# Two modulation chunks of the last channel group: summed on VectorE instead of TensorE

## The chip, the cores and the metric

The kernel runs on one core of a Trainium2 chip, in one launch. The metric is the device time of that launch in microseconds. TensorE (PE in the profile) multiplies matrices, VectorE (DVE), ScalarE (ACT) and GpSimd (POOL) work on tiles, and SyncE (SP) issues all transfers from the chip's memory, in one queue.

## The reference

Two layers of a diffusion backbone over 256 latent and 256 context tokens of width 2048, in float32. What matters here is the start of the first layer:

```python
silu_c, silu_cc = jax.nn.silu(c), jax.nn.silu(c_ctx)
ml = (silu_c @ w_mod[i] + b_mod[i]).reshape(B, 6, 1, D)      # latent
mc = (silu_cc @ w_mod[i] + b_mod[i]).reshape(6, 1, 1, D)     # context
a_lat = modulate(rms_norm(h, norm1_g[i]), ml[:, 0], ml[:, 1])
y_lat = pool_mix(a_lat, pool_w[j], pool_b[j], pool_scale[j])
h = h + ml[:, 2] * y_lat
h = h + ml[:, 5] * conv_ffn(modulate(rms_norm(h, norm2_g[i]), ml[:, 3], ml[:, 4]), ...)
```

The same is done for the context tokens with `mc`. `pool_mix` subtracts each token from a windowed mean (windows 2, 4, 8, 16 for four groups of 512 channels) and multiplies each group by a 512x512 matrix. The second layer is neighbourhood attention with its own feed-forward part.

The modulation is a product of two vectors (latent and context) with a matrix of 2048 x 12288, 100 MB: six parts of 2048 columns. The kernel cuts these into 24 chunks of 512 columns. Chunk `4 * part + group` holds part `part` of channel group `group`; the parts are shift 1, scale 1, gate 1, shift 2, scale 2, gate 2. So group four (number 3 in the code) needs chunks 3, 7, 11 for its mixer, 19 (its second scale) for the operands `Ad` of its share of the feed-forward product, and 15 (its second shift) for a correction term.

## The kernel before

All tiles have channels on the 128 partitions. A float32 weight is split into a high and a low part (`split`: ScalarE makes the high one, VectorE the low one), and a product is three matmuls of 512 columns, both streams of tokens side by side.

The first stretch runs over the four channel groups (called one to four here, `g` = 0 to 3 in the code). For each group:

- `mod_pe` sums a chunk on TensorE: 8 tiles of 1024 columns are loaded, each serves two matmuls with 32 output rows (`mod`); ScalarE copies the result (`modev`), TensorE transposes it (`modt`, four transposes), VectorE reduces it to `modT` and adds the bias (`finish_mod`).
- `mixer(g)` forms the pooled operands: `py`, `ws` and `pf` on VectorE and GpSimd, `ph` as high and low part, then TensorE's `pm` matmuls; ScalarE scales (`pz`), GpSimd adds to the residual `hl`, `hc`. At its end it writes `Ad`, the residual times the second scale, as high and low part.
- `partial(g)` multiplies this group's `Ad` with its share of the first eight blocks of the gate and up weights (`cg`, `cu`); VectorE adds the results into `part`. `early_shifts` multiplies the second shift (tile `sh`, copied from `modT` of chunks 12 to 15 by `shifts`) with the same weights (`pw`), summed by VectorE into `shsum`.

While `partial(g)` runs, the function `between`, called 32 times in each group, pumps the chunks of group `g + 1` (`need`), steps `mixer(g + 1)`, and in group four normalises the residual (`n2s`, `n2d`, `n2b`, `nrm`, `A`) and starts the first gates (`g`, `sg`, `late`). The order in which each engine gets its instructions is fixed when the program is built, by a scheduler that may move an instruction ahead of others written before it; each engine then works strictly in that order.

Weights go through a ring of staging tiles of 512 KB (`stage`): six of its own, and those of the 16 tiles `A0` to `A15` (operands of the products) that a group doesn't hold, lent by `lend`. A load waits in SP's queue until its staging tile has been read.

The four second gates (chunks 20 to 23) and the second layer's chunks are summed later on VectorE (`mod_pieces`), with `scalar_tensor_tensor` steps (weight times a per-partition scalar, plus the sum so far), 32x32 transposes, reductions, and a small matmul with `quad`, a stack of four identities.

Of the kernel before, what the change touches and what calls it, by code (L numbers as in the profile page):

```python
# [17 lines left out]
P = 128  # L18
# [40 lines left out]
def kernel(ctx: ExitStack, tc: tile.TileContext, xT, cxT, wmod, wg, wu, wd, wp,  # L59
# [50 lines left out]
    def lend(ks):  # L110

        rooms[:] = [r for r in rooms if r in RING or r in ks] + [k for k in ks if k not in rooms]
# [49 lines left out]
    def finish_mod(l, ch, mt):  # L162

        which, q = divmod(ch, 4)
        mt2 = flat(mt)
        nc.vector.tensor_tensor(mt2, mt2, V(f"bm_{l}")[:, 8 * ch : 8 * ch + 8], op=ALU.add)
        if which in (1, 4):
            nc.vector.scalar_tensor_tensor(mt2, mt2, 1.0, V(f"g{1 if which == 1 else 2}_{l}")[:, 8 * q : 8 * q + 8],
                                           op0=ALU.add, op1=ALU.mult)
        modT[l, ch] = mt  # L170

    def mod_pe(chs, sc, pool):

        ps = bank("m", f"mod{chs[0]}")
        for c, ch in enumerate(chs):
            for g in range(4):
                ts = load(lambda a, b: wmod[0, ch, g, :, a:b], 2048, f"wm0_{ch}_{g}")
                for j in range(4):
                    at = 32 * (4 * g + j) + 30 - 2 * c
                    nc.tensor.matmul(ps[32 * j : 32 * j + 32, :], sc[:, at : at + 32],  # L180
                                     ts[j // 2][0][:, 512 * (j % 2) : 512 * (j % 2) + 512],
                                     start=(c == 0 and g == 0), stop=(ch == chs[-1] and g == 3),
                                     tile_position=(0, 32 * j))
                if ch == chs[-1] and g == 3:
                    ev = pool.tile([P, 512], F32, tag="t2", name=f"modev{ch}")
                    nc.scalar.copy(ev, ps)
                yield
        with tc.high_priority():
            p2 = bank("d", f"modt{ch}")
            for i in range(4):  # L190
                nc.tensor.transpose(p2[:, P * i : P * i + P], ev[:, P * i : P * i + P], ident)
        for c, ch in enumerate(chs):
            r = main.tile([P, 4, 2], F32, name=f"modT0_{ch}")
            nc.vector.tensor_reduce(out=r, in_=by_row(p2, 2 * c), axis=AX.X, op=ALU.add)
            finish_mod(0, ch, r)

    m0 = main.tile([P, 4, 4, 2], F32, name="modT0")
    for q in range(4):
# [177 lines left out]
    with ExitStack() as ph0:  # L376
# [56 lines left out]
        with ExitStack() as phs:  # L433
# [36 lines left out]
            def mods():  # L470

                for g in range(4):
                    for chs in ([g, 4 + g], [8 + g], [16 + g], [12 + g]) if g else ([4], [0], [8], [16], [12]):
                        yield from mod_pe(chs, sc, f0)
                    shifts(g)
            pump0 = mods()
            done = [0]

# [210 lines left out]
            for n in (0, 8, 11, 15, 15, 17, 17):  # L689
                need(n)  # L690
                next(mix)
            rstd = None
            BACK = {(2, 31): range(4, 8), (3, 9): range(8, 12), (3, 17): ()}
            for g in range(4):
                lend((range(8, KT), [*range(12, KT), *range(4)], range(8), range(4, 12))[g])
                mix = mixer(g + 1) if g < 3 else None
                todo = [20 * g + 20 + n for n in STEPS] if g < 3 else []
                last = [14]
                F = {}
                rstd = n2.acc  # L700

                def between(half):
                    need(min(20 * g + LEAD + RATE * (half + 1) // 32, 20 * g + LEAD + PMAX))
                    if (g, half) == (0, 4):
                        next(first)
                    if (g, half) in BACK:
                        lend(BACK[g, half])
                    if g == 3 and half == NRH:
                        nc.scalar.copy(rstd, n2.rstd())
                        late_norm.append(rstd)  # L710
                    if todo and done[0] > todo[0] and half >= last[0] + 2:
                        last[0] = half
                        todo.pop(0)
                        next(mix)
                    k = (half - NRH) // 2
                    if g == 3 and 0 <= k < 12 and (half - NRH) % 2 == 0:
                        normalise(0, 3, h_of, both, rstd, f0, range(k, k + 1), keep=F)
                    e = (half - 14) // 2
                    if g == 3 and half % 2 == 0 and 0 <= e < 8:
                        nc.sync.dma_start(home[e // 2][:, :, e % 2], h_of(e % 2)[:, 4 * (e // 2) : 4 * (e // 2) + 4, :])  # L720
                    if g == 3 and half in GATES:
                        e = GATES.index(half)
                        acts[e], _ = gate0(e, *late(e))

                partial(g, shs[g % 2], between)
                for n in todo:
                    need(n)
                    next(mix)
            need(81)
            nbank[0] = 0  # L730
            A.update(F)

# [641 lines left out]
```

## Time and profile before

| | |
|---|---|
| runs (us) | 3066.27, 3069.55, 3070.97; median 3069.55 |
| profiled execution | 3071.95 us, its span 3070.2 us |
| TensorE busy | 2980.5 us (97%) |
| VectorE busy | 2048.8 us (67%) |
| ScalarE, GpSimd busy | 1346.4 us (44%), 827.3 us (27%) |
| read from the chip's memory | 559.12 MB |

Busy times are sums over the whole span. In the rows of the profile each group of instructions is named by its line in the kernel, the tile it writes and the tiles it reads, without the numbers of the tiles; `x32` counts instructions. A square bracket tells how long the engine was idle before the instruction, and what released it. A matmul's end is modelled, and matmuls overlap, so their cadence is read from their starts. A modulation matmul shows as two records. PEclk is the clock that TensorE was granted, as a share of full speed. The first stretch ends at about 425 us.

### The profile page before, as it was taken

How to read it: one execution, taken by the hardware profiler on the slowest of the kernel's cores; microseconds unless marked ns; L12 is line 12 of the kernel's file. 1: busy time of each engine (PE TensorE's matmuls, PEld its weight loads, DVE VectorE, ACT ScalarE, POOL GpSimd, SP SyncE). 2: the span in 40 equal slices, each digit the busy share in tenths (PEclk: the TensorE clock that was granted, in tenths of full speed). 3: DMA queues.
4: the chain of work that ended last, by engine and by line, in shares of the span. 5: the costliest groups of instructions: out<-in, count | busy, mean ns of one | idle time of the engine just before them, and what ended most of it. 6: DMA issues, size and time to landing. Idle time of an engine off the chain costs nothing.

```text
span 3070.2 us, 40370 instructions
## 1 busy us (share of the span) xinstructions
PE 2980.5 (97%) x14828; PEld 2399.6 (78%) x14828; DVE 2048.8 (67%) x2845; ACT 1346.4 (44%) x2193; POOL 827.3 (27%) x787
## 2 busy tenths in 40 slices
PE   6999889999999999999999999999999999999998
PEld 2565568888888888888887888878888888888887
DVE  4445786584876868587686666474777666666666
ACT  3333463323333232333334444343545666656665
POOL 1011310303123030321403000000002466556665
PEclk9999999999999999999999999999999999999999
DMA  9989424464855857676672333333345556555563
GB/s 356 329 326 332 163 83 154 159 202 137 256 184 190 250 177 238 192 228 195 208 239 91 108 113 103 105 113 103 109 158 184 179 183 201 189 189 180 185 192 117
DMA packets 183302, 568.07 MB, mean 185 GB/s; under 512 B 17856, under 2 KB 26560, under 8 KB 183104
## 3 DMA queue, kind: packets, MB, share of 16 engines
q1 hardware_dynamic: 183104, 565.49, 56.5%
q8 instruction: 117, 1.92, 0.2%
q14 instruction: 81, 0.66, 0.1%
HBM read 559.12 MB, written 6.29 MB: 184 GB/s over the span
## 4 chain that ended last, share of the span: by engine, by line
PE 85%; issue 5%; DVE 5%; DMA 2%; POOL 1%; ACT 1%; SPq 0%; DVEq 0%; POOLq 0%; ACTq 0%
PE g L915 5%; PE u L915 5%; PE d L799 5%; PE d L801 5%; PE d L800 5%; PE d L962 4%; PE u L777 4%; PE u L775 4%; PE u L776 4%; PE g L777 4%; PE g L775 4%; PE g L776 4%; PE g L918 3%; PE u L918 3%; PE d L966 2%
## 5 line engine op out<-in xcount | busy, mean ns | idle before, releaser
L819 POOL TENSOR_TENSOR hl<-hl,dy 128x256 f32<-128x256 f32 x144 | 138.0, 958 | 963.3 <-ACT dy L816 685.3
L977 POOL TENSOR_TENSOR hl<-hl,dy 128x256 f32<-128x256 f32 x320 | 331.5, 1071 | 188.3 <-ACT dy L975 186.1
L258 DVE SCALAR_TENSOR_TENSOR macc<-wm,sc,macc 128x512 f32<-128x512 f32 x360 | 261.4, 776 | 8.6 <-DMA wm<-wmod 8.3
L239 DVE SCALAR_TENSOR_TENSOR macc<-wm,sc,macc 128x1024 f32<-128x1024 f32 x120 | 160.1, 1334 | 70.3 <-DMA wm<-wmod 69.2
L816 ACT ACTIVATE dy<-d,modT 128x256 f32<-128x256 f32 x224 | 93.6, 471 | 141.8 <-PE d L801 139.8
L819 POOL TENSOR_TENSOR hc<-hc,dy 128x256 f32<-128x256 f32 x144 | 141.4, 982 | 0.0
L975 ACT ACTIVATE dy<-d,modT 128x512 f32<-128x512 f32 x160 | 104.5, 684 | 42.8 <-PE d L966 41.4
L180 PE MATMUL mod<-wm,sc 128*32 128x512 f32 x640 | 96.0, 631 | 19.9 <-DMA wm<-wmod 19.9
L1064 POOL TENSOR_TENSOR rk<-rk,rp 128x256 f32<-128x256 f32 x16 | 13.7, 858 | 362.8 <-DVE rk L1063 265.9
L146 DVE TENSOR_TENSOR wd_2l<-wd,wd_2h 128x1024 fp32r<-128x1024 f32 (+1 forms) x44 | 58.2, 1332 | 68.4 <-ACT wd_2h L144 68.4
L417 ACT ACTIVATE sg<-g 128x512 f32<-128x512 f32 x43 | 27.2, 632 | 161.4 <-DVE g L414 161.2
L146 DVE TENSOR_TENSOR wd_3l<-wd,wd_3h 128x1024 fp32r<-128x1024 f32 (+1 forms) x44 | 53.9, 1248 | 65.0 <-ACT wd_3h L144 65.0
L502 POOL TENSOR_TENSOR pf<-ws,inv 128x256 f32<-128x256 f32 x32 | 28.3, 905 | 206.6 <-DVE ws L494 193.1
L144 ACT CAST wd_0h<-wd 128x1024 fp32r<-128x1024 f32 (+1 forms) x44 | 45.2, 1031 | 77.7 <-PE g L776 47.6
L146 DVE TENSOR_TENSOR wd_1l<-wd,wd_1h 128x1024 fp32r<-128x1024 f32 (+1 forms) x44 | 55.8, 1272 | 31.4 <-ACT wd_1h L144 31.4
L146 DVE TENSOR_TENSOR wd_0l<-wd,wd_0h 128x1024 fp32r<-128x1024 f32 (+1 forms) x44 | 54.9, 1254 | 23.5 <-ACT wd_0h L144 23.5
L941 DVE TENSOR_TENSOR actb<-sgb,actb 128x256 fp32r<-128x256 f32 x43 | 52.3, 1216 | 27.0 <-ACT actb L940 27.0
L1152 ACT ACTIVATE sb<-sb,nm 128x512 f32<-128x512 f32 x64 | 46.2, 722 | 52.7 <-DVE nm L1148 52.2
L799 PE MATMUL d<-act,wd_0h 128*128 128x512 f32 x172 | 68.0, 395 | 1.0 <-ACT dy L816 1.0
L144 ACT CAST wd_1h<-wd 128x1024 fp32r<-128x1024 f32 (+1 forms) x44 | 45.0, 1027 | 53.8 <-PE u L776 25.3
L801 PE MATMUL d<-act,wd_3l 128*128 128x512 f32 x172 | 67.8, 394 | 0.4 <-DVE wd_3l L146 0.4
L799 PE MATMUL d<-act,wd_3h 128*128 128x512 f32 x172 | 68.2, 396 | 0.0
(1702 smaller groups left out, 9339.1 us busy)
## 6 DMA issues: line engine op xcount, KB each, us to landing
wm<-wmod SPq DMA_DIRECT2D x384, 512.0 KB, 6.0
wd<-wd SPq DMA_DIRECT2D x168, 512.0 KB, 4.5
wg<-wg SPq DMA_DIRECT2D x156, 512.0 KB, 4.6
wu<-wu SPq DMA_DIRECT2D x156, 512.0 KB, 4.6
wv<-wv SPq DMA_DIRECT2D x32, 512.0 KB, 3.7
wk<-wq SPq DMA_DIRECT2D x32, 512.0 KB, 3.9
wq<-wq SPq DMA_DIRECT2D x32, 512.0 KB, 3.8
wo<-wo SPq DMA_DIRECT2D x32, 512.0 KB, 4.5
```

The source lines that it names most:

```text
L146: eng.tensor_tensor(lo[:, :n], t[:, :n], hi[:, :n].bitcast(F32), op=ALU.subtract)
L239: nc.vector.scalar_tensor_tensor(acc, w, sc2[:, k, 0:1], acc, op0=ALU.mult, op1=ALU.add)
L258: nc.vector.scalar_tensor_tensor(acc[:, s], w, sc2[:, k, s : s + 1], acc[:, s], op0=ALU.mult, op1=ALU.add)
L775: nc.tensor.matmul(ps, hi[:, c : c + P], xh, start=(k == 0), stop=False)
L776: nc.tensor.matmul(ps, hi[:, c : c + P], xl, start=False, stop=False)
L777: nc.tensor.matmul(ps, lo[:, c : c + P], xh, start=False, stop=(k == KT - 1))
L799: nc.tensor.matmul(ps, hi[:, o : o + P], xh, start=(i == 0), stop=False)
L801: nc.tensor.matmul(ps, lo[:, o : o + P], xh, start=False, stop=(i == n - 1))
L819: nc.gpsimd.tensor_tensor(h_of(s)[:, k, :], h_of(s)[:, k, :], y[:, s], op=ALU.add)
L915: nc.tensor.matmul(ps, hi[:, c : c + P], flat(B[k]), start=(k == 0), stop=False)
L918: nc.tensor.matmul(ps[:, T:], lo[:, c : c + P], B[k][:, 0], start=False, stop=(k == KT - 1))
L977: nc.gpsimd.tensor_tensor(hl[:, k, :], hl[:, k, :], y[:, q], op=ALU.add)
```

## The change

Chunks 15 and 19 no longer go through `mod_pe`. A new generator, `mod_pair`, loads for each of the 16 blocks of 128 input channels the 512 columns of both chunks into one staging tile (`wm0p`), and VectorE adds them, times the latent and times the context vector, to two sums (`mpacc`). At the end it transposes and reduces the sums, one matmul (`modp`) adds over the partitions, and eight small copies make `modT` of both chunks. `between` steps it at each third call in groups two and three; it needs 20 steps of 22, after which `shifts(3)` copies `sh`. The sums and a work tile (`mproom`, with its own copy of `quad`) take `A1`, `A2`, `A3` in these two groups, so that 11 staging tiles are left in place of 14. The pump counts 73 steps where it counted 81.

```diff
+    def mod_pair(chs):
+        acc = [ap0.tile([P, 1024], F32, tag=f"A{2 + s}", name=f"mpacc{s}") for s in both]
+        room = ap0.tile([P, 1024], F32, tag="A1", name="mproom")
+        quad = room[:, 0:P].rearrange("p (j c) -> p j c", j=4)
+        sums = room[:, P : P + 64].rearrange("p (c s k) -> p c s k", c=2, s=2)
+        for k in range(KT):
+            g, kk = divmod(k, 4)
+            w = stage(f"wm0p_{k}")
+            step = chs[1] - chs[0]
+            nc.sync.dma_start(w.rearrange("p (c n) -> p c n", c=2),
+                              wmod[0, chs[0] : chs[1] + 1 : step, g, :, 512 * kk : 512 * kk + 512]
+                              .rearrange("c p n -> p c n"))
+            for s in both:
+                if k == 0:
+                    nc.vector.tensor_scalar(acc[s], w, sc2[:, k, s : s + 1], None, op0=ALU.mult)
+                else:
+                    nc.vector.scalar_tensor_tensor(acc[s], w, sc2[:, k, s : s + 1], acc[s], op0=ALU.mult, op1=ALU.add)
+            yield
...
+        for s in both:
+            t = room[:, 512:1024]
+            for c in range(2):
+                nc.vector.transpose(t, acc[s][:, 512 * c : 512 * c + 512])
+                nc.vector.tensor_reduce(out=sums[:, c, s], in_=t.rearrange("p (k r) -> p k r", r=32), axis=AX.X, op=ALU.add)
+            yield
+        ps = bank("d", f"modp{chs[0]}")
+        nc.tensor.matmul(ps[:, 0:64], room[:, 0:P], room[:, P : P + 64], start=True, stop=True)
...
@@ mods
-                    for chs in ([g, 4 + g], [8 + g], [16 + g], [12 + g]) if g else ([4], [0], [8], [16], [12]):
+                    for chs in ([g, 4 + g], [8 + g], *(([16 + g], [12 + g]) if g < 3 else ())) if g else ([4], [0], [8], [16], [12]):
                         yield from mod_pe(chs, sc, f0)
-                    shifts(g)
+                    if g < 3:
+                        shifts(g)
@@ the loop over groups
+            pair = [mod_pair((15, 19))]
-                lend((range(8, KT), [*range(12, KT), *range(4)], range(8), range(4, 12))[g])
+                lend((range(8, KT), [0, *range(12, KT)], [0, *range(4, 8)], range(4, 12))[g])
...
+                    if g in (1, 2) and half % 3 == 0 and pair:
+                        if next(pair[0], "done") == "done":
+                            pair.clear()
+                            shifts(3)
...
-            need(81)
+            need(73)
```

The order of the instructions moves with it. The first place is VectorE's queue near the end of group three's mixer (`ph` of its last two tiles), before:

```order
L503 TENSOR_TENSOR pf_1724<-pf_1724,pad_201 128x512
L576 TENSOR_TENSOR gbi_1626<-gsc_1625,vt 128x8
L494 TENSOR_TENSOR ws_1784<-pad_203 128x2x271
L508 TENSOR_TENSOR ph_1732<-pf_1724,ph_1732 128x512
L494 TENSOR_TENSOR ws_1784<-ws_1784 128x2x269
L677 TENSOR_TENSOR part_901<-part_901,cu_4_1763 128x512
L494 TENSOR_TENSOR ws_1784<-ws_1784 128x2x265
L503 TENSOR_TENSOR pf_1783<-pf_1783,pad_203 128x512
L508 TENSOR_TENSOR ph_1791<-pf_1783,ph_1791 128x512
```

and the same place on VectorE now:

```order
L214 SCALAR_TENSOR_TENSOR mpacc_1313<-wm0p_1859,sc_81,mpacc_1313 128x1024
L214 SCALAR_TENSOR_TENSOR mpacc_1314<-wm0p_1859,sc_81,mpacc_1314 128x1024
L534 TENSOR_TENSOR ws_1823<-pad_203 128x2x271
L548 TENSOR_TENSOR ph_1767<-pf_1759,ph_1767 128x512
L534 TENSOR_TENSOR ws_1823<-ws_1823 128x2x269
L214 SCALAR_TENSOR_TENSOR mpacc_1313<-wm0p_1990,sc_81,mpacc_1313 128x1024
L214 SCALAR_TENSOR_TENSOR mpacc_1314<-wm0p_1990,sc_81,mpacc_1314 128x1024
L534 TENSOR_TENSOR ws_1823<-ws_1823 128x2x265
L543 TENSOR_TENSOR pf_1822<-pf_1822,pad_203 128x512
L548 TENSOR_TENSOR ph_1830<-pf_1822,ph_1830 128x512
```

Two pairs of the new steps stand among the last rows of the mixer; six more such steps stand further up, between the `modT` of chunks 2 and 6 and here.

The second place is TensorE's queue around the transposes of chunks 2 and 6 (`modt`) in group two, before:

```order
L664 MATMUL cg_4_1573<-Ad_1296,wcg_4h_1555 128x512
L665 MATMUL cg_4_1573<-Ad_1296,wcg_4h_1555 128x512
L666 MATMUL cg_4_1573<-Ad_1296,wcg_4l_1556 128x512
L664 MATMUL cg_953<-Ad_1275,wcg_4h_1559 128x512
L665 MATMUL cg_953<-Ad_1275,wcg_4h_1559 128x512
L666 MATMUL cg_953<-Ad_1275,wcg_4l_1560 128x512
L664 MATMUL cg_953<-Ad_1280,wcg_4h_1559 128x512
L191 MATMUL modt_1580<-ident,modev_1542 128x128 x4
```

(the last row follows three more of the same `cg`), and the same place on TensorE now:

```order
L665 MATMUL pw_2_1590<-wcg_4_0_1578,sh_207 32x256
L665 MATMUL pw_2_1590<-wcg_4_1024_1580,sh_207 32x256
L191 MATMUL modt_1607<-ident,modev_1569 128x128 x4
L706 MATMUL cg_4_1600<-Ad_1275,wcg_4l_1583 128x512
L704 MATMUL cg_4_1600<-Ad_1280,wcg_4h_1582 128x512
L705 MATMUL cg_4_1600<-Ad_1280,wcg_4h_1582 128x512
L706 MATMUL cg_4_1600<-Ad_1280,wcg_4l_1583 128x512
```

The transposes moved ahead of ten matmuls of `cg_4` and seven of the next `cg`.

The third place is VectorE's queue at the start of group four's normalisation, before:

```order
L350 TENSOR_SCALAR n2d<-ident,n2v 128x128 x4
L146 TENSOR_TENSOR wcu_0l_2872<-wcu_0_1024_2865,wcu_0h_2871 128x1024
L194 TENSOR_REDUCE modT_15_2804<-modt_2799 128x8
L363 SCALAR_TENSOR_TENSOR nrm_2785<-hl,modT_16_533,n2acc 128x256
L363 SCALAR_TENSOR_TENSOR nrm_2785<-hc,modT_16_533,n2acc 128x256
L166 TENSOR_TENSOR modT_15_2804<-modT_15_2804,vt 128x8
```

and now:

```order
L146 TENSOR_TENSOR wcu_0l_2879<-wcu_0_1024_2872,wcu_0h_2878 128x1024
L389 TENSOR_SCALAR n2d<-ident,n2v 128x128 x4
L402 SCALAR_TENSOR_TENSOR nrm_2801<-hl,modT_16_533,n2acc 128x256
L402 SCALAR_TENSOR_TENSOR nrm_2801<-hc,modT_16_533,n2acc 128x256
L402 SCALAR_TENSOR_TENSOR nrm_2823<-hl,modT_16_533,n2acc 128x256
```

The rows of chunk 15 are gone from it (they, and the copy of `sh`, now stand in group three), and the split `wcu_0l` stands ahead of `n2d`, no longer behind it. In TensorE's queue the eight `mod` tiles of chunk 15, which stood between group four's last `pm` and its first `cg`, are gone, and so are those of chunk 19 among the `cu` and `pm` before.

More of the change, by code (lines that the diff above doesn't have):

```diff
@@ L195, in mod_pe @@
             finish_mod(0, ch, r)
+    def mod_pair(chs):
[16 more added lines that the diff above has]
+            yield
+        nc.vector.tensor_reduce(out=quad[:, 0], in_=ident.rearrange("p (j c) -> p c j", j=4), axis=AX.X, op=ALU.add)
+        for j in range(1, 4):
+            nc.vector.tensor_copy(quad[:, j], quad[:, 0])
+        for s in both:
[6 more added lines that the diff above has]
+        nc.tensor.matmul(ps[:, 0:64], room[:, 0:P], room[:, P : P + 64], start=True, stop=True)
+        v = ps[:, 0:64].rearrange("p (c s i b) -> p c s i b", c=2, s=2, b=4)
+        for c, ch in enumerate(chs):
+            r = main.tile([P, 4, 2], F32, name=f"modT0_{ch}")
+            for b in range(4):
+                own = slice(32 * b, 32 * b + 32)
+                nc.vector.tensor_copy(r[own].rearrange("p i s -> p s i"), v[own, c, :, :, b])
+            finish_mod(0, ch, r)
+        yield
     m0 = main.tile([P, 4, 4, 2], F32, name="modT0")
```

## The prediction

> **What bounds the kernel now.** I read the utilisation by stage first, because the change touches one stretch of some 200 us in a run of 3070 us, then TensorE's waits in that stretch, then the timelines of TensorE and VectorE around the places where the work is added or taken away, and last the DMA queue.
>
> ```profile
> core 0: us, PE busy (x) PEld busy (x) DVE busy (x) ACT busy (x) POOL busy (x), PEclk, DMA share, GB/s
> 165.00:215.00 50.00, 48.74 (x296) 30.39 (x294) 22.62 (x35) 15.93 (x32) 6.86 (x8) 1.00 0.84 301
> 215.00:246.00 31.00, 31.00 (x171) 19.33 (x171) 25.83 (x44) 11.88 (x18) 7.86 (x8) 1.00 1.00 382
> 246.00:264.00 18.00, 16.86 (x94) 10.50 (x93) 12.38 (x19) 12.58 (x28) 6.34 (x8) 1.00 0.87 315
> 264.00:300.00 36.00, 36.00 (x220) 20.55 (x218) 11.84 (x20) 3.74 (x4) 0.00 (x0) 1.00 0.89 315
> 300.00:337.00 37.00, 37.00 (x186) 22.36 (x186) 29.62 (x50) 11.88 (x18) 7.09 (x8) 1.00 0.81 301
> 337.00:357.00 20.00, 17.80 (x101) 11.60 (x99) 11.46 (x20) 13.09 (x29) 7.24 (x9) 1.00 0.33 105
> 357.00:368.00 11.00, 5.01 (x26) 3.45 (x30) 10.42 (x24) 5.98 (x14) 2.72 (x2) 0.91 0.00 1
> 368.00:400.00 32.00, 31.92 (x173) 23.61 (x166) 24.87 (x38) 15.48 (x30) 12.07 (x8) 0.92 0.29 99
> 400.00:425.00 25.00, 12.06 (x54) 9.76 (x54) 25.00 (x44) 14.94 (x28) 4.96 (x3) 0.78 0.39 126
> ```
>
> Each row is a stretch, its length, and then busy us of the engines. Groups two and three are about 165 to 264 and 264 to 349 us, group four follows. TensorE (PE) works without a break to 337 us. VectorE (DVE) has room in 165:215 (27.4 us idle) and 264:300 (24.2 us idle), but hardly any in 215:246 (31 - 25.83 = 5.2 us idle), where it forms the pooled operands of group three. From 400 on VectorE is the full one.
>
> ```profile
> PE g L775 <- DVE late L401: 12.9, 1, 12.9
> PE pw L625 <- ACT A L365: 4.7, 1, 4.7
> ```
>
> These are TensorE's two longest waits from 100 to 430 us. No row names a wait for a modulation weight: in this stretch the loads come ahead of TensorE. So taking matmuls away pays only where TensorE, and not VectorE's chain, sets the end.
>
> **The work that TensorE loses.**
>
> ```profile
> 344.33 3.64 PE L180 MATMUL mod<-wm,sc 128*32 128x512 f32 x32
> 349.34 0.50 PE L665 MATMUL cg<-Ad,wcg_0h 128*128 128x512 f32 x1 [0.68 <-DVE Ad L606]
> 343.75 0.66 PE L191 MATMUL modt<-ident,modev 128*128 128x128 f32 x4 [0.72 <-ACT modev L186]
> ```
>
> The 32 records in 3.64 us are all of chunk 15; the four transposes are 0.6 us. A chunk is thus 4.2 us of TensorE, two are 8.5 us. What comes in is one f32 matmul of 64 columns, which I cost at 0.2 us or less (each of those transposes of 128 columns is 0.15). Two copies of 512 columns on ScalarE go too; they had cover, so zero. Chunk 15 filled the time in which TensorE waited anyway: right behind it `cg` still waits 0.68 us for `Ad`. Its 4.2 us I count at nothing (at most -4.2): without it TensorE waits for `Ad` sooner. Chunk 19's 4.2 us lies between 319 and 334 us, beside VectorE's chain for group four's mixer.
>
> **The work that VectorE gains.**
>
> ```profile
> L239 DVE SCALAR_TENSOR_TENSOR macc<-wm,sc,macc x120: 1271/1285/1859, 802.9 to 1609.5; 128x1024 f32<-128x1024 f32 x120
> L213 DVE STREAM_TRANSPOSE modu<-macc x40: 662/684/706, 528.9 to 1632.2; 128x512 f32<-128x512 f32 x40
> L237 DVE TENSOR_SCALAR macc<-wm,sc x8: 739/745/748, 801.1 to 1570.0; 128x1024 f32<-128x1024 f32 x8
> L214 DVE TENSOR_REDUCE modr<-modu 128x16 f32<-128x512 f32 x16 | 10.1, 666 | 0.0
> L468 DVE COPY sh<-modT x1: 159/159/159, 367.0 to 367.0; 128x8 f32<-128x8 f32 x1
> ```
>
> The same forms run later in this kernel (min/median/max ns): 30 x 1.285 + 2 x 0.745 + 4 x 0.684 + 4 x 0.666 = 45.4 us, and some 13 small copies and reductions of about 0.16 us, 2 us. Of the 32 large steps the new order puts six ahead of group two, six in 165:215, ten into the mixer of group three, two among group three's `Ad`, and eight, with the folds, behind it. The first, second and last of these sets fit into the idle time just read. The ten do not: 25.83 + 10 x 1.285 = 38.7 us in a stretch of 31.
>
> ```profile
> 215.08 0.29 DVE L194 TENSOR_REDUCE modT<-modt 128x8 f32<-128x32 f32 x2 [1.34 <-PE modt L191]
> 243.31 0.69 DVE L503 TENSOR_TENSOR pf<-pf,pad 128x512 f32<-128x512 f32 x1 [1.61 <-POOL pf L502]
> 244.69 0.69 DVE L508 TENSOR_TENSOR ph<-pf,ph 128x512 fp32r<-128x512 f32 x1 [0.69 <-ACT ph L507]
> 249.43 0.74 POOL L595 TENSOR_TENSOR hl<-hl,pz 128x256 f32<-128x256 f32 x1 [6.16 <-ACT pz L593]
> ```
>
> This chain runs from `modT` at 215.1 to the last `ph` at 245.4, and TensorE's `pm`, GpSimd's additions to `hl` and the `Ad` of group three stand behind it. Full of work, it grows by 38.7 - 31 = **+7.7 us**. Against that its start moves: in the new order the transposes of chunks 2 and 6 stand ahead of 17 `cg` matmuls that they followed.
>
> ```profile
> 150.40 0.40 PE L666 MATMUL cu<-Ad,wcu_4l 128*128 128x512 f32 x1
> 150.63 0.40 PE L664 MATMUL cu<-Ad,wcu_4h 128*128 128x512 f32 x1
> ```
>
> A matmul starts each 0.23 us, so 17 are 3.9 us. **Group three's boundary: +7.7 - 3.9 = +3.8 us**, between -3.9 (the steps fit into waits) and +7.7 (no earlier start).
>
> **End of group three.** The transposes of chunks 3 and 7 likewise come ahead of ten `cg` matmuls, seven `pw` and the first `mod` of chunk 11: 10 x 0.23 + about 1.6 = 3.9 us earlier start of group four's mixer. From there VectorE is busy 29.62 of 37 us and sets the end; the copies of the pair add 1.4 us to it. TensorE, 4.2 us lighter by chunk 19, follows. **-2.5 us**; bounds -8.1 (3.9 and 4.2 both count) and +1.4 (no earlier start).
>
> **Group four.**
>
> ```profile
> 357.24 0.87 DVE L350 TENSOR_SCALAR n2d<-ident,n2v 128x128 f32<-128x128 f32 x4
> 358.02 1.22 DVE L146 TENSOR_TENSOR wcu_0l<-wcu,wcu_0h 128x1024 fp32r<-128x1024 f32 x1
> 367.02 0.16 DVE L468 COPY sh<-modT 128x8 f32<-128x8 f32 x1
> 367.28 1.10 PE L625 MATMUL pw<-wcg,sh 128*32 128x256 f32 x8 [4.74 <-ACT A L365]
> DVE part L677 <- PE cu L666: 3.8, 2, 2.0
> DVE part L677 <- PE cg L666: 3.1, 1, 3.1
> ```
>
> `pw` reads `sh`, whose copy from chunk 15's `modT` VectorE does at 367.02, behind twelve `nrm` steps; 0.1 us later `pw` starts. (The view names ScalarE, which ended last; the copy fits better.) Now `sh` is ready long before, and the 4.74 us go. They count, because VectorE later waits 3.8 + 3.1 us for TensorE's `cu` and `cg` (its waits from 357 to 425). But one `wcu_0l` of 1.22 us now stands ahead of `n2d`. **-3.5 us**; bounds -4.7 and 0.
>
> **The loads.** The 16 loads of the pair, 0.52 MB each, move from about 290-335 us into 150-290.
>
> ```profile
> DMA packets 15312, 43.88 MB, mean 325 GB/s; under 512 B 1349, under 2 KB 3525, under 8 KB 15300
> GB/s 343 17 274 368 341 351 401 355 374 412 341 215 66 311 358 393 405 411 411 409 277 330 385 411 411 386 353 125 299 354 336 319 402 393 276 169 87 320 401 410
> SPq L128 <- PE mod L180: 57.6, 23, 8.8
> ```
>
> All are of 165 to 300 us. 43.88 + 8.39 MB in 135 us are 387 GB/s; the best slices show 411, so it just fits. SP stood 57.6 us because tiles were still read by TensorE: the loads were ahead. With 11 staging tiles in place of 14 they are less so. I take **+1 us**. If the queue idled as much as now (the shares 0.84, 1.00, 0.87 and 0.89 of the four stages above make 14.3 us idle in 135), 16 x 1.28 = 20.4 us would leave it 6.1 us behind: that is the upper end, 0 the lower.
>
> **Sum**: +3.8 - 2.5 - 3.5 + 1.0 = -1.2 us against the profiled execution's 3071.95 us, which lies 2.4 us above the median of the runs, 3069.55. I predict 3069.55 - 1.2 = **3068.4 us**. 0.2% (6.1 us) is about what a measurement of this kernel can tell from no change.
>
> **Rivals.** *Faster*: VectorE's ten steps slip into its waits for GpSimd and ScalarE (1.61 and 0.69 us rows above, 5.2 in all) and the scheduler's new order puts other splits later, so that group three's boundary costs nothing; at the end of group three chunk 19's 4.2 us count, and group four gives its 3.5: -7.7 us, 3061.9. For it: TensorE has no idle time before 337 us, the mark of an engine that sets the pace. Against: 38.7 us in 31.
>
> *Slower*: the loads. Sixteen more transfers stand in SP's queue ahead of chunks 2, 6, 3 and 7. It decides as soon as they land after TensorE reaches them; then neither transpose comes early (+3.9 and +3.9), and the queue's lag goes up from 1 to 6.1: -1.2 + 7.8 + 5.1 = +11.7 us, 3081.3. For it: 387 of 411 GB/s and three tiles fewer. Against: 57.6 us of SP waiting because it was ahead.
>
> *The port*: the added steps slow GpSimd, or are slowed by it.
>
> ```profile
> L565 DVE SCALAR_TENSOR_TENSOR py<-hl,modT,rs x4: 472/722/962, 215.8 to 235.4; 128x256 f32<-128x256 f32 x4
> 234.37 2.54 POOL L502 TENSOR_TENSOR pf<-ws,inv 128x256 f32<-128x256 f32 x2 [3.79 <-DVE modT L166]
> 235.36 0.96 DVE L565 SCALAR_TENSOR_TENSOR py<-hl,modT,rs 128x256 f32<-128x256 f32 x1
> 241.84 1.44 POOL L502 TENSOR_TENSOR pf<-ws,inv 128x256 f32<-128x256 f32 x2 [4.93 <-DVE ws L494]
> ```
>
> One form takes 0.47 or 0.96 us, the latter beside GpSimd's `pf`, whose pair took 2.54 us there and 1.44 alone. If the last `pf` pair meets two added steps, the chain grows by 2 x 1.285 = 2.6 us: 3071.0. The Trainium skill, "SBUF — State Buffer", section "Who interferes with whom", says that a VectorE instruction with two SBUF inputs contends with a GpSimd one that reads SBUF, and that the second to issue blocks entirely. The added step has two SBUF inputs; by that rule each meeting costs the whole of the other's duration, and the sum would be 3071.0 or more, where by undisturbed rows it is 3068.4. The trace agrees with the rule in the rows of `py`.
>
> **Chances.** My forecast, with its own spread of 6 us to either side, 0.42; the faster rival 0.30, the slower 0.22, the port 0.06. Splitting each at 6.1 us: faster 0.04 + 0.27 = 0.31; same 0.34 + 0.03 + 0.02 + 0.04 = 0.43; slower 0.04 + 0.20 + 0.02 = 0.26. The range reaches from a little beyond the faster rival, 3060, to the slower one, 3082.
>
> **What the profile after would show.** If the boundary term is right, TensorE waits 3 us or more for `pm` or `Ad` between 245 and 270 us, and VectorE is above 9 tenths there. If the start terms are right, `modT` of chunks 2 and 3 come about 4 us sooner after the last `mod` than now. In group four the wait of `pw` is gone. A wait of TensorE or VectorE for `wm` or `wm0p` from DMA speaks for the slower rival. I would be wrong if VectorE stands for a load with evictions behind it (`part`, the splits, `shsum`): a single such stop holds TensorE's banks too.

## The result: 0.86% slower, and the profile after

| | before | changed |
|---|---|---|
| median of the runs (us) | 3068.47 | 3094.97 (3090.37 to 3102.06) |
| ratio, 95% interval | | 1.0086 [1.0073, 1.0098] |
| profiled execution, its span | 3071.95, 3070.2 | 3096.06, 3094.3 |

The change costs 26 us. I had forecast 3068.4, no change, with a range up to 3082. (The median before is 3069.55 for three runs and 3068.47 with a fourth.)

The loss is best located by TensorE's first `cg` matmul of each group: the distance between two of them is one group's stage. By that measure group one (its `cg` to that of group two) grew from 93.2 to 94.7 us, group two from 84.9 to 101.3, group three went from 89.1 to 89.2, and group four (to the first matmul of the next stretch) from 76.4 to 83.4. Two thirds of the loss is in group two. Its stage in the view of busy times by stretch, before and then now (the columns are those of the stage table above):

```profile
core 0: us, PE busy (x) PEld busy (x) DVE busy (x) ACT busy (x) POOL busy (x), PEclk, DMA share, GB/s
173.93:258.88 84.95, 83.73 (x480) 52.08 (x480) 51.27 (x82) 28.81 (x53) 15.54 (x18) 1.00 0.92 344
```

```profile
175.50:276.70 101.20, 95.81 (x472) 52.10 (x472) 67.55 (x98) 26.79 (x50) 12.82 (x17) 0.98 0.93 325
```

VectorE has 16 us more to do, as planned. But TensorE is busy 12 us more with eight records fewer, and 8 of these 12 us are the matmuls of the modulation. The same two stretches with `mod` alone (TensorE, its weight loads, ScalarE):

```profile
173.93:258.88 84.95, 21.09 (x160) 4.31 (x160) 2.31 (x4) 1.00 0.92 344
```

```profile
175.50:276.70 101.20, 29.01 (x152) 4.60 (x152) 2.32 (x4) 0.98 0.93 325
```

The DMA share is 0.92 before and 0.93 now. The bytes of the two stages, from the DMA view:

```profile
DMA packets 10044, 29.26 MB, mean 344 GB/s; under 512 B 907, under 2 KB 2218, under 8 KB 10037
```

```profile
DMA packets 12120, 32.86 MB, mean 325 GB/s; under 512 B 1008, under 2 KB 2160, under 8 KB 12112
```

3.6 MB more went through this stage. At the old 344 GB/s they alone would be 10.5 of its 16.3 us. What became of `mod` is seen in TensorE's timeline, before and then now (last bracket: idle time before, and who released it):

```profile
217.56 1.06 PE L180 MATMUL mod<-wm,sc 128*32 128x512 f32 x8
```

```profile
178.06 1.92 PE L180 MATMUL mod<-wm,sc 128*32 128x512 f32 x4 [1.85 <-DMA wm<-wmod]
...
214.09 2.34 PE L180 MATMUL mod<-wm,sc 128*32 128x512 f32 x16 [0.17 <-DMA wm<-wmod]
216.80 0.59 PE L665 MATMUL pw<-wcg,sh 128*32 128x256 f32 x2 [0.37 <-DMA wcg<-wg]
...
223.33 1.05 PE L180 MATMUL mod<-wm,sc 128*32 128x512 f32 x4
```

One load is read by two matmuls (four records), and each of these writes 32 of the 128 output rows; the load beside it serves the other 64 rows. Where both stand together in TensorE's queue, the records for different rows start within 0.02 us of each other, and all eight take 1.06 us. One load alone takes 1.05. Before, nearly all loads of this stage stand in pairs; now 16 of 38 stand alone, between other matmuls. Fourteen of the 16 had landed 3.6 us or more before TensorE read them (worked out from the order of the loads in the program and their landings in the trace). So these cost TensorE time by their place in its queue, and not by a wait.

The row at 178.06 has another cause besides: the granted clock was 0.50 there.

```profile
177.80:181.20 3.40, 3.14 (x7) 1.29 (x8) 3.16 (x8) 0.92 (x3) 0.00 (x0) 0.50 0.95 304
```

Some weights do arrive only as they are read, as at 178.06 and 214.09. TensorE's and ScalarE's waits for loads from 100 to 460 us show it; first before, then now (the longest):

```profile
ACT wcu_4h L144 <- DMA wcu<-wu: 12.2, 4, 8.0
PEld mod L180 <- DMA wm<-wmod: 1.6, 5, 0.4
```

```profile
ACT wcg_4h L144 <- DMA wcg<-wg: 27.8, 3, 27.3
ACT wcu_0h L144 <- DMA wcu<-wu: 11.0, 3, 6.7
PEld mod L180 <- DMA wm<-wmod: 7.5, 10, 2.3
DVE mpacc L214 <- DMA wm0p<-wmod: 4.2, 2, 2.5
PE mod L180 <- DMA wm<-wmod: 2.9, 3, 1.8
```

And this is what SP, which issues the loads, waits for between 165 and 300 us now:

```profile
SPq L128 <- PE mod L180: 32.3, 20, 4.8
SPq L207 <- PE mod L180: 25.8, 8, 6.5
SPq L128 <- DVE mpacc L214: 11.7, 7, 3.0
```

Line 207 is the pair's load. Each of these is a wait for a staging tile that has not been read yet. The 57.6 us of this kind before have become 32.3 + 25.8, and VectorE's steps hold tiles for another 11.7.

The chain on VectorE in group three's mixer, from `modT` of chunk 2 to the last `ph`:

```profile
221.46 0.28 DVE L194 TENSOR_REDUCE modT<-modt 128x8 f32<-128x32 f32 x2
...
223.57 2.47 DVE L214 SCALAR_TENSOR_TENSOR mpacc<-wm0p,sc,mpacc 128x1024 f32<-128x1024 f32 x2
...
262.66 0.69 DVE L543 TENSOR_TENSOR pf<-pf,pad 128x512 f32<-128x512 f32 x1 [1.60 <-POOL pf L542]
264.04 0.69 DVE L548 TENSOR_TENSOR ph<-pf,ph 128x512 fp32r<-128x512 f32 x1 [0.68 <-ACT ph L547]
```

It takes 43.3 us where it took 30.3. Five pairs of steps, 2.47 us each, are 12.4 of the 13.0. The waits of 1.60 and 0.68 us at the end are those of before: the steps did not slip into them.

With this chain, group two's stage falls into three parts: from its first `cg` to `modT` of chunk 2, the chain, and from the last `ph` to the next group's first `cg`. The last three rows are experiments that follow.

| us | to `modT` | chain | to `cg` | stage |
|---|---|---|---|---|
| before | 41.2 | 30.3 | 13.5 | 85.0 |
| changed | 46.0 | 43.3 | 12.0 | 101.3 |
| e1, loads, 11 tiles, no steps | 44.0 | 34.3 | 20.3 | 98.6 |
| e3, 11 tiles, nothing else | 51.8 | 31.4 | 17.2 | 100.4 |
| e8, loads, 14 tiles | 58.2 | 31.6 | 18.4 | 108.2 |

In the changed kernel the chain with its steps is 13.0 of the 16.3 us. The three experiments are as slow in this stage, but elsewhere in it.

### The profile page after: what moved, and what is told of

The parts are those of the page before. It is cut to its first block, busy times and chain, and to the rows that moved or that the text cites. A ratio compares the mean times of both kernels' runs of the same rounds, so it can differ in the third digit from the quotient of the medians.

```text
span 3094.3 us, 40254 instructions
## 1 busy us (share of the span) xinstructions
PE 2991.6 (97%) x14758; PEld 2400.5 (78%) x14758; DVE 2096.7 (68%) x2895; ACT 1346.0 (43%) x2191; POOL 825.1 (27%) x787
## 4 chain that ended last, share of the span: by engine, by line
PE 86%; DVE 5%; issue 5%; DMA 2%; POOL 1%; ACT 1%; SPq 0%; DVEq 0%; ACTq 0%; POOLq 0%
PE g L960 5%; PE u L960 5%; PE d L844 5%; PE d L846 5%; PE d L845 5%; PE d L1007 4%; PE u L822 4%; PE u L820 4%; PE u L821 4%; PE g L822 4%; PE g L820 4%; PE g L821 4%; PE g L963 3%; PE u L963 3%; PE d L1011 2%
## 5 line engine op out<-in xcount | busy, mean ns | idle before, releaser
L146 DVE TENSOR_TENSOR wd_2l<-wd,wd_2h 128x1024 fp32r<-128x1024 f32 (+1 forms) x44 | 58.2, 1331 | 67.2 <-ACT wd_2h L144 67.2
L845 PE MATMUL d<-act,wd_2h 128*128 128x512 f32 x172 | 68.1, 396 | 0.0
```

The lines of the kernel that those rows point to most:

```text
L146: eng.tensor_tensor(lo[:, :n], t[:, :n], hi[:, :n].bitcast(F32), op=ALU.subtract)
L845: nc.tensor.matmul(ps, hi[:, o : o + P], xl, start=False, stop=False)
```

## The experiments

All ratios are to the kernel before, run on the same chip. Times are medians.

### The parts one at a time

```diff
@@ e1: mod_pair, its 30 large steps
-                    nc.vector.scalar_tensor_tensor(acc[s], w, sc2[:, k, s : s + 1], acc[s], ...)
+                    nc.vector.scalar_tensor_tensor(acc[s][:, 0:8], w[:, 0:8], sc2[:, k, s : s + 1], acc[s][:, 0:8], ...)
@@ e2: mod_pair, one load
-            w = stage(f"wm0p_{k}")
+            w = room
+            if k == 0:
                 nc.sync.dma_start(w..., wmod[0, ...])
@@ e3: the kernel before
-                lend((range(8, KT), [*range(12, KT), *range(4)], range(8), range(4, 12))[g])
+                lend((range(8, KT), [0, *range(12, KT)], [0, *range(4, 8)], range(4, 12))[g])
@@ e4: the changed kernel, between
-                    if g in (1, 2) and half % 3 == 0 and pair:
-                        if next(pair[0], "done") == "done": ...
+                    if (g, half) == (2, 27):
+                        modT[0, 15], modT[0, 19] = modT[0, 14], modT[0, 18]
+                        shifts(3)
@@ e4: lend as before
```

> The changed kernel with its 16 loads, its 11 staging tiles and its fold, but each of the 30 large VectorE steps cut from 1024 to 8 columns (chunks 15 and 19 are then wrong sums): some 38 us of VectorE's work are gone, all else stays. VectorE theory (the five pairs of steps in group three's mixer, 12.4 us, and the pairs beside GpSimd's additions at 165 us, 2 us, are the loss): 3095 - 14 = about 3080 or less, and if only the 4.4 us by which modT of chunk 2 is late are left, 3076. Transfer theory (16 more loads and three tiles fewer make the weights late, and TensorE waits): 3088 to 3095, modT of chunk 2 still at about 221 us.

> The changed kernel with one load of the pair in place of 16: all 32 steps read that one tile, which lies in A1 (chunks 15 and 19 are then wrong sums). VectorE's work, the 11 staging tiles and the fold stay, 7.9 MB of transfers are gone. VectorE theory: 3087 to 3095 (at most the 4.4 us of late weights come back, and modT of chunk 2 is at 215 to 217 us). Transfer theory: 3075 or less.

> The kernel before, chunks 15 and 19 on TensorE as ever, but with 11 staging tiles in groups two and three in place of 14. Both theories in their simple form: 3068 to 3070, no change, since SP waited for tiles with loads far ahead. If the tiles and not the added bytes make the weights late: 3073 to 3076, modT of chunk 2 some 4 us later.

> Chunks 15 and 19 are taken off TensorE and not summed at all (the sums of 14 and 18 stand in for them); 14 staging tiles, no added step, no added load. It is the most that the change could win. If TensorE's 8.5 us set the end: 3060 to 3061. My sum without the terms of the added work (boundary -3.9, end of group three -3.9, group four -3.5) says 3058. If the removed matmuls stood in time in which TensorE waits for VectorE, ScalarE and GpSimd anyway: 3065 to 3069.

| | us | ratio, 95% interval |
|---|---|---|
| e1, loads, 11 tiles, no steps | 3091.32 | 1.0068 [1.0056, 1.0080] |
| e2, steps, 11 tiles, one load | 3089.83 | 1.0062 [1.0050, 1.0074] |
| e3, 11 tiles, nothing else | 3089.71 | 1.0063 [1.0051, 1.0075] |
| e4, nothing added, 14 tiles | 3071.09 | 0.9999 [0.9990, 1.0007] |

Each theory held in one run and fell in the other: e1 lies in the range of transfers, e2 in that of VectorE. Taking away the steps gave back some 5 us, taking away the loads some 7 (the intervals still touch that of the changed kernel). In e2, though, the steps no longer wait for loads, and the scheduler put eleven of the 32 into group one, whose stage is 103.7 us. And e3, which I had put in as a formality, loses 19 us with the work of the kernel before untouched: three staging tiles alone cost some three quarters of what the whole change does. Its stages are 93.0, 100.4, 94.5 and 76.3 us: group two grew by as much as in the changed kernel, but by a later `modT` (table above). TensorE there, and the stretch behind its stop:

```profile
211.40 1.92 PE L180 MATMUL mod<-wm,sc 128*32 128x512 f32 x4 [5.82 <-DMA wm<-wmod]
```

```profile
209.50:219.70 10.20, 7.56 (x30) 1.55 (x32) 2.36 (x2) 2.48 (x3) 0.00 (x0) 0.50 0.69 243
```

The granted clock is 0.50 from within this stop of 5.82 us to 219.7 us, so the stop costs more than its length. (Such a stretch of 10.2 us at 0.50 stands at the stops of 5.84, 5.78 and 6.45 us in e8, e15 and e18 too; group two of the kernel before has neither.) Group two of e3 in the busy times and in the DMA view:

```profile
170.45:270.85 100.40, 91.57 (x484) 53.43 (x481) 52.42 (x87) 30.03 (x58) 15.18 (x17) 0.95 0.82 292
```

```profile
DMA packets 9993, 29.27 MB, mean 292 GB/s; under 512 B 902, under 2 KB 2147, under 8 KB 9986
```

The same 29.3 MB, but the share has fallen to 0.82: loads could not be issued. In this stage SP waits 40.9 us for tiles that `mod` has yet to read, 26.5 before. Worked out from issue, landing and first read of each `wm` load issued from 165 to 265 us: before, 48 loads took 8.3 us to land and then lay 13.6 us until TensorE read them; in e3, 42 loads took 7.7 and lay 10.8. A tile is taken for some 20 us per load, so the number of tiles over that time is an estimate of the rate of loads.

e4 shows that there was nothing to win that the runs could tell from no change. Its group three is 6.5 us shorter (82.5), its group four 2.7 us longer (79.2). Part of both is the measure: chunk 15's 3.64 us ran ahead of group four's first `cg`, so they counted in group three. The 3.8 us that the two stages gain together in the profiled execution are not seen in the median of the runs, which spread from 3065 to 3074 us.

### The order of the loads

In e3 the tile that TensorE waits for at 211.40, the last half of chunk 6, was issued behind seven halves of chunk 10. So I took the order of SP's queue for the cause.

```diff
@@ e5, e6, e7: load, and the pair's load; e9 to e12: in load, for wm tiles alone
+            with tc.issue_after(<the load written before>):
                 nc.sync.dma_start(t[:, :n], src(j, j + n))
@@ e8: mod_pair: no sums, no fold, all 14 tiles
+        acc = [flat(main.tile([P, 4, 2], F32, name=f"modT0_{ch}")) for ch in chs]
...
+                    nc.vector.scalar_tensor_tensor(acc[s], w[:, 0:8], sc2[:, k, s : s + 1], acc[s], ...)
```

> The changed kernel, but in the first stretch each load into a staging tile is held behind the load written before it, so that SP issues them in the order in which the code asks for them. In the changed kernel SP's order is another: the second half of a tile of chunk 6 lands 33 us before TensorE reads it, while the last tile of chunk 13, read 30 us earlier, lands behind it at 178.01 and is read at 178.06. Order theory (11 tiles make the scheduler put loads out of turn, and TensorE waits for the ones put back): 3072 to 3080, modT of chunk 2 back at 215 to 217 us. Depth theory (11 tiles cannot run far enough ahead, whatever the order): 3090 to 3097.

> The kernel before with 11 staging tiles in groups two and three, loads issued in written order. Order theory: 3068 to 3074, where the same without the fixed order gave 3089.7. Depth theory: 3086 to 3092.

> The kernel before, all 14 tiles, loads issued in written order. Both theories: 3066 to 3073; if the order that the scheduler chose with 14 tiles is worth something by itself, slower than 3073.

> The changed kernel with all 14 staging tiles: the 16 loads stay where they are, but the sums, the work tile and the fold are gone, and each load is read only by two VectorE steps of 8 columns (chunks 15 and 19 are then wrong sums). It differs from the loads-only kernel (3091.3) by the three tiles and the fold's 6 us. Depth theory: 3070 to 3074 (the added bytes alone cost 0 to 6.1 us, as in my upper bound). If the 16 loads are by themselves enough to put the order out: 3080 to 3091.

> The changed kernel, with only TensorE's modulation loads (wm) held in the order in which TensorE reads them; the loads of wcg, wcu, wp and wm0p stay free to go ahead of them or behind. Out-of-turn theory (in every kernel that lost 18 us or more with free loads, a wm tile that TensorE reads first stands in SP's queue behind wm tiles that it reads 10 to 33 us later, lands last and is read 0.04 us after it lands): 3075 to 3085, the loss of 26 us at least halved, and no wm lands less than 1 us before its use. Depth theory (fewer tiles, or more loads through them, cannot run far enough ahead): 3090 to 3100, no change.

> The kernel before with 11 staging tiles in groups two and three and the wm loads held in turn. Out-of-turn theory: 3070 to 3078 (3089.7 without the hold). Depth theory: 3087 to 3092.

> The 16 loads with two small VectorE steps each, 14 staging tiles, no sums and no fold (chunks 15 and 19 are wrong sums), and the wm loads held in turn. Out-of-turn theory: 3072 to 3082 (3099.5 without the hold). Depth theory: 3096 to 3102.

> The kernel before, all tiles, with the wm loads held in turn. There too some wm loads stand out of turn (the first half of a tile of chunk 6 is issued behind its other seven halves), but none lands less than 2.3 us before its use. Both theories: 3066 to 3072, no change.

| ratio (us) | free order | wm in turn | all in written order |
|---|---|---|---|
| kernel before | 1 | 1.0051 (3085.16) | 1.0115 (3105.25) |
| 11 tiles | 1.0063 (3089.71) | 1.0111 (3103.46) | 1.0150 (3116.38) |
| loads, 14 tiles | 1.0096 (3099.48) | 1.0090 (3096.31) | |
| changed | 1.0086 (3094.97) | 1.0113 (3103.75) | 1.0177 (3124.95) |

No forecast of the order theory came true: a held order makes the kernel before slower by 16 and 35 us, and none of the others faster beyond its interval. But the depth theory's ranges were passed too, in all of these runs but e11, and these runs can't decide between the two, since the hold changed something else. Group two's stage, the busy time of `mod` in it, and TensorE's idle time (stage less busy time):

| us | free order | wm in turn | all in written order |
|---|---|---|---|
| kernel before | 85.0, 21.1, 1.2 | 92.3, 26.7, 1.6 | 97.8, 31.9, 0.0 |
| 11 tiles | 100.4, 27.9, 8.8 | 99.6, 33.1, 2.1 | 103.5, 34.2, 2.8 |
| loads, 14 tiles | 108.2, 30.2, 12.8 | 99.0, 30.8, 2.7 | |
| changed | 101.3, 29.0, 5.4 | 102.6, 31.9, 5.0 | 106.9, 32.8, 7.0 |

With the `wm` loads in turn, the stops of the runs with 11 tiles and with the 16 loads do shrink, from 8.8 and 12.8 to 2.1 and 2.7 us. But the hold also parted `mod` matmuls that stood in pairs, and in the kernel before these alone take 5.6 of the 7.3 us by which the stage grew. So loads out of turn may well cause the stops; whether they, or too few tiles whatever the order, is not shown. Within each order three tiles fewer cost 19, 18 and 11 us and the whole change 26, 19 and 19.

e8 was the second surprise: the 16 loads alone, with all tiles and hardly a VectorE step, cost 29 us, where I had bounded them at 6.1. It is above both of its ranges.

### How many tiles

```diff
@@ the kernel before: lend in groups two and three
+ e13: [*range(12, KT), *range(3)], [*range(3), *range(4, 8)]
+ e14: [*range(12, KT), *range(2)], [*range(2), *range(4, 8)]
+ e15: [*range(12, KT), 0], range(8)
@@ e16: the changed kernel
+ lend: [0, *range(8, KT)], [0, *range(4, 8), *range(12, KT)]
+ BACK: (1, 10): [0, *range(12, KT)], (2, 10): [0, *range(4, 8)]
```

> The kernel before with 13 staging tiles in groups two and three (A3 is not lent). Depth theory (all tiles are held all the time, 23.6 us each from issue to last read, so that loads per us are tiles over hold time, and each tile less costs the same): 3069.5 + 19.3 / 3 = 3076, range 3073 to 3079. Order-by-luck theory (any edit gives SP's queue another order, and the order before is a lucky one): anywhere between 3068 and 3095, with no regard to the number of tiles.

> The kernel before with 12 staging tiles in groups two and three (A2 and A3 are not lent). Depth theory: 3069.5 + 2 x 6.4 = 3082, range 3079 to 3086, and above the run with 13 tiles. Order-by-luck theory: anywhere between 3068 and 3095; equal to or below the run with 13 tiles in one case of two.

> The kernel before with 11 staging tiles in group two, and all 14 again in group three. Depth theory: the loss of the run with 11 in both (19.3 us) lay by 12 us ahead of modT of chunk 2, so 3080 to 3086. If group three's tiles are as dear: 3076 to 3080.

> The changed kernel, but in the first ten of the 32 calls of between in groups two and three the four tiles that the next group's mixer will want (A8 to A11 in group two, A12 to A15 in group three) are lent as well, so that there are 15 staging tiles, then 11. Depth theory: a good half of the tile loss comes back, 3078 to 3087. If VectorE's steps or the bytes are what is left of the loss: 3090 to 3096.

| | us | ratio, 95% interval |
|---|---|---|
| e13, 13 tiles | 3072.42 | 1.0008 [0.9999, 1.0017] |
| e14, 12 tiles | 3076.66 | 1.0022 [1.0014, 1.0031] |
| e3, 11 tiles | 3089.71 | 1.0063 [1.0051, 1.0075] |
| e15, 11 in group two alone | 3085.15 | 1.0048 [1.0035, 1.0060] |
| e16, changed, 15 then 11 | 3099.70 | 1.0104 [1.0088, 1.0119] |

The loss goes with the number: 2.5, 6.8 and 19 us for one, two and three tiles, the first of which its interval can't tell from nothing. That speaks against any edit's luck with the order; but it isn't 6.4 us a tile either, e13 and e14 lie below their ranges, and the third costs most. Three quarters lie in group two (e15), as expected. e16 missed: four tiles more in the first third of a group did not help (its group two stage is 100.9 us). Tiles that must be given back before the mixer are gone when the loads for it are due; I have not shown that this is the reason.

### The steps alone, and the loads with another reader

```diff
@@ e17: mod_pair, no load, 13 tiles
+        acc = ap0.tile([P, 1024], F32, tag="A3", name="mpacc")
+                nc.vector.scalar_tensor_tensor(acc, acc, sc2[:, k, s : s + 1], acc, ...)
@@ e18: e8 with GpSimd as the reader
+                    nc.gpsimd.tensor_tensor(acc[s], w[:, 0:8], acc[s], op=ALU.add)
```

> Chunks 15 and 19 are off TensorE, no load of the pair, no fold, and VectorE does 32 steps of the same form and size on one tile in A3, in place (chunks 15 and 19 are wrong sums); 13 staging tiles. VectorE's work by itself, to be read against the run with 13 tiles (3072.4) and the run with nothing added (3071.1). If VectorE's steps lengthen group three's mixer as in the changed kernel (+13 us): 3082 to 3087. If the tiles and loads explain the whole loss: 3069 to 3075.

> The kernel with the 16 loads and 14 staging tiles (3099.5), with the two 8-column steps on each load given to GpSimd in place of VectorE (chunks 15 and 19 are wrong sums); SP's order is the same but for two rows. If the loads cost because VectorE stood for them (28.9 us in seven or eight waits) with the mixer's and the eviction's steps behind: 3075 to 3085. If they cost as transfers and tiles held: 3096 to 3101.

e17: 3081.61 us, 1.0039 [1.0027, 1.0052], between the two ranges: VectorE's steps alone cost 12 us, 9.2 more than 13 tiles do. But their place is not the one expected: group one's stage grew from 93.2 to 104.3 us, group two's only from 84.9 to 89.4. Without loads to wait for, eight steps stand ahead of the `Ad` of group two, beside GpSimd's additions (VectorE's timeline, then GpSimd's); so e17 doesn't price the steps where the changed kernel has them.

```profile
162.48 5.97 DVE L203 SCALAR_TENSOR_TENSOR mpacc<-mpacc,sc 128x1024 f32<-128x1024 f32 x4
...
181.29 0.47 DVE L619 SCALAR_TENSOR_TENSOR Ad<-hl,modT,Ad 128x256 fp32r<-128x256 f32 x1
```

```profile
165.65 1.72 POOL L608 TENSOR_TENSOR hc<-hc,pz 128x256 f32<-128x256 f32 x1
```

The first `Ad` of group two began on VectorE at 173.7 us in the kernel before.

e18: 3098.71 us, 1.0095 [1.0080, 1.0111], the same as e8. VectorE no longer stands for `wm0p` (21.9 and 7.0 us in e8); GpSimd does, for 90.9 us (e8, then e18):

```profile
DVE modT L211 <- DMA wm0p<-wmod: 21.9, 7, 7.3
```

```profile
POOL modT L211 <- DMA wm0p<-wmod: 90.9, 13, 12.4
...
ACT wcu_0h L144 <- DMA wcu<-wu: 41.5, 2, 20.8
...
PEld mod L180 <- DMA wm<-wmod: 14.8, 11, 6.9
```

GpSimd's waits seem to hold up nobody: in group two (172 to 282 us) VectorE and ScalarE wait for GpSimd 4.7 us in all, and 5.4 in the kernel before (172 to 280 us). So the loss does not hang on VectorE as the reader: the loads seem to cost as transfers, through the tiles and the place in the queue that they take from `wm` and `wcu`. e8's group two in the DMA view:

```profile
DMA packets 12639, 34.06 MB, mean 315 GB/s; under 512 B 1045, under 2 KB 2197, under 8 KB 12631
```

4.8 MB more than before in a stage of 108.2 us, 23 us longer.

## Why the prediction was wrong

**The loads (+1, bounds 0 and 6.1): the step that failed.** Three tiles fewer cost 19 us, the loads alone 29. Three readings were at fault. First, "SP stood 57.6 us because tiles were still read by TensorE: the loads were ahead". They were ahead by 13.6 us on average, but SP's wait says that the ring was full: the tiles held the loads back, and I took tiles away. Second, the bound let the 16 loads fill all of the 14.3 us in which the queue idled in 135. The average hid that group two's stage already ran at a share of 0.92. It is at 0.93 now, so none of its idle time was used, though the stretch 215:246 of the prediction's table shows that the queue can run at 1.00 for 31 us. Third, "no row names a wait for a modulation weight" was read from TensorE's matmuls alone: its weight loads waited 1.6 us for `wm` before, and ScalarE 12.2 us for `wcu` (the waits shown with the result). Chunks 15 and 19 had been loaded in group three's stage, which before had this share, 0.76:

```profile
258.88:347.93 89.05, 87.20 (x481) 51.60 (x481) 51.81 (x86) 27.36 (x49) 12.64 (x16) 1.00 0.76 271
```

**The boundary of group three (+3.8): the other step, +16.3 measured.** Counted from the stage's start, `modT` of chunk 2 came 4.8 us later, not 3.9 sooner. The last `mod` ahead of the transposes ended 5.3 us later, for the reasons shown with the result. From its end to `modT` the new order gained 0.5 us (5.0 against 5.5): ScalarE waited until 216.8 us for a tile of `wcg`, whose splits stood ahead of `modev` on ScalarE and of `modT` on VectorE. The chain behind it grew by 13.0 where I had 7.7, since no idle time was filled; the rest of the stage gave back 1.5. So the steps are the largest part of this loss, and still e1 and e3, without them, have nearly the same stage: their `modT` or their end comes later.

**The end of group three (-2.5): +0.1 measured.** The start failed here too: `modT` of chunk 3 came 43.5 us into the stage, 40.9 before, and not 3.9 sooner. The chain from there to the last `ph` grew by 4.3, where I had 1.4 for the copies. From the last `ph` to the next `cg` the stage lost 6.7 us, of which chunk 15's matmuls, no longer there, are 4.2. 11 tiles alone lengthen the stage by 5.5 (e3).

**Group four (-3.5).** The wait of `pw` is gone as forecast: it now follows its `cg` directly. But the stage is 7.0 us longer. `cg` starts right behind the last `pm` and then waits for `Ad`, which chunk 15's 3.64 us had covered; and `n2d` is late.

```profile
370.10 0.73 PE L704 MATMUL cg<-Ad,wcg_0h 128*128 128x512 f32 x2 [1.08 <-ACT Ad L645]
372.29 0.74 PE L705 MATMUL cg<-Ad,wcg_0h 128*128 128x512 f32 x1 [1.45 <-DVE Ad L646]
...
382.57 2.06 PE L391 MATMUL n2b<-n2d,ones 128*128 128x512 f32 x2 [2.95 <-DVE n2d L389]
...
388.02 1.09 PE L665 MATMUL pw<-wcg,sh 128*32 128x256 f32 x16
...
394.52 1.09 PE L665 MATMUL pw<-wcu,sh 128*32 128x256 f32 x16 [2.42 <-DVE part L717]
...
397.32 0.80 PE L704 MATMUL cu<-Ad,wcu_0h 128*128 128x512 f32 x1 [1.71 <-DVE shlast L674]
```

And the 4.74 us of `pw` came back right behind it, as 2.42 and 1.71 us in which the next `pw` and the next `cu` wait for VectorE. VectorE sets the pace here, so a wait taken from TensorE was not a gain.

Chunk 15's 4.2 us I had counted at nothing, and e4 bears that out. Its leaving makes the stage, as measured here, 2.7 to 3.6 us longer (e2, e4, e17); in every run with the 16 loads and free order it is 5 to 8 us (e1, e8, e16, e18 and the changed kernel). What the loads, which end by 304 us, do to a stage that begins at 366 is open. The granted clock has a part in it: over this stage it is 0.87 in the changed kernel, 0.84, 0.81, 0.85 and 0.88 in e1, e8, e16 and e18, and 0.89 before; but e18 is 5 us longer at nearly the old clock.

**The rivals.** The slower one came nearest: neither transpose came early, and its sign, waits for `wm` and `wm0p`, is there (7.5, 2.9 and 4.2 us above). But its condition, weights that land as TensorE reaches them, holds for some loads alone. Its price of 11.7 us rested on the same bound of 6.1 and left out the chain's idle time, the parted `mod` matmuls and the clock; its chance of 0.22 rested on reading SP's wait as evidence against it. The faster one took TensorE's unbroken work for the mark of the engine that sets the pace; e4 takes 8.5 us from TensorE, and the median stays. The port is real, but not at `pf`: four added steps meet GpSimd's additions at 165 us, in the changed kernel (VectorE, then GpSimd) and before (GpSimd):

```profile
165.09 6.31 DVE L214 SCALAR_TENSOR_TENSOR mpacc<-wm0p,sc,mpacc 128x1024 f32<-128x1024 f32 x4 [1.72 <-DMA wm0p<-wmod]
```

```profile
165.16 1.81 POOL L635 TENSOR_TENSOR hl<-hl,pz 128x256 f32<-128x256 f32 x1 [15.26 <-ACT pz L633]
```

```profile
165.36 0.74 POOL L595 TENSOR_TENSOR hl<-hl,pz 128x256 f32<-128x256 f32 x1 [15.26 <-ACT pz L593]
```

GpSimd's addition takes 1.7 to 1.8 us in place of 0.74, the step 1.58 in place of 1.285; group two's start is 1.5 us later, this being a part of it. The Trainium skill, "SBUF — State Buffer", section "Who interferes with whom", has the second of the two block entirely. These rows agree that the two contend, most of the cost falling on GpSimd, but not with a full block: one after the other a step and an addition would take 1.285 + 0.74 = 2.0 us, and here such a pair takes 1.6 to 1.8.

**What stays open.** The costs don't add: tiles 19, loads 29 and steps 9 to 12 make 26 together. I read the three parts of the stage so: TensorE is busy for 42.5 of the chain's 43.3 us, so VectorE's steps run beside a TensorE that its parted `mod` matmuls keep as long, and taking one away uncovers the other (e1: chain 9 us shorter, end 8 longer). That is an argument, not a measurement; a kernel with the matmuls held in pairs would test it. Why the loads cost less with 11 tiles (e1, 21 us for both) than with 14 (e8) is not settled; each kernel gets its own order, and in the held order the loads cost 12 us and the tiles 18. No version beat the kernel before, and e4 leaves nothing measurable for one on this path.

## What to carry to other kernels

Before taking buffers from a ring of loads, read who the issuing queue waits for: if it waits for readers of the buffers, the ring is full, and a shorter one can hold the loads back. (Its length over the time that one load is held estimates the rate of loads, but not the loss: by it each tile would have cost 6.4 us, where one cost 2.5 and three 19.) Price added loads in the stage where they land, at the share that this stage already has, not against the idle time of an average. Where an engine's busy time grows without more work, look at the place of its instructions in the queue and at the granted clock before calling it a wait. And run the change with its benefit only, nothing added: here that would have shown at once that 8.5 us of TensorE were worth nothing measurable.

## What was unexpected of the hardware

TensorE's busy time held a loss that no wait names: in group two `mod` took 29.01 us for 152 records against 21.09 for 160. One load's four records take 1.05 us, and two loads' eight, side by side in the queue, 1.06. A stop of TensorE can cost more than its length: with one of 5.82 us in e3 the granted clock stood at 0.50 up to 8 us after its end. And one tile of 14 cost 2.5 us (not clear of nothing), the third 12: the ring had a little slack, and then none.
